# Head norms of a retention branch: the inverse root by ScalarE's root, or by a bit guess and three Newton steps on VectorE

## The chip, the cores and the metric

The kernel runs on one NeuronCore of a Trainium2 chip. The engines named here are TensorE (PE in the profile; its weight loads are PEld), VectorE (DVE), ScalarE (ACT), GpSimd (POOL) and the DMA queues that SyncE issues (SP, SPq). Each engine takes its instructions in the order in which they were written into its queue. The metric is the time of one execution in device microseconds.

## The reference, cut to what matters

One decoder layer is computed for a prompt of 1024 tokens and for 8 samples of 4 tokens. Its input projection feeds two branches: sparse attention (8 heads, the 256 best keys by an indexer), and retention (8 heads). The change lies in the norm of the retention heads. Each head's 64 outputs of a token are brought to mean 0 and variance 1, and then gated:

```python
def _head_norm(o):
    mu = jnp.mean(o, axis=-1, keepdims=True)
    var = jnp.mean(jnp.square(o - mu), axis=-1, keepdims=True)
    return (o - mu) * lax.rsqrt(var + EPS)

    ob, sp = _retention(qb, kb, vb, ...)           # chunks of 128 tokens, state carried on
    yb = jax.nn.silu(gb) * _head_norm(ob)
    y = jnp.einsum('btd,...', concat(ya, yb), w_out)
```

Everything is in float32.

## The kernel before, in words

The kernel is written as tiles and instructions for named engines. A planner turns the program text into one queue for each engine: it plays the program through on a model of the chip (`schedule_with_timeline_sim=True`, line 2002), and whenever an engine is free there, it takes the ready instruction that comes first in the program text, or one that was marked as urgent. So the order in a queue depends on the modelled times of everything ahead of it.

Stages, in order of time: norms of the inputs, the projections for the indexer and attention, the index scores and the search for the thresholds; then the retention stage with the sample branch's key selection; then attention; then the output projection and the gate.

In the retention stage the heads are worked in four pairs (`for hp in range(4)`, line 1566). For each pair:

- `pqk`: eight blocks of 128 tokens are projected to q and k (`mm_a`, lines 287 to 289, 24 matmuls a block), turned by the rotary angle on VectorE (`rope`, lines 1116 to 1118) and finished on GpSimd (1120, 1121).
- `pvg`: the same eight blocks are projected to v and the gate. `take_vg` (1129, 1131) scales v and computes the gate's SiLU on ScalarE.
- The retention itself, block by block (`chunk_mm` and lines 1605 to 1618): q and k are transposed, copied (`qkT`, line 1142), multiplied, masked on VectorE (`sm`, 1148), joined with the carried state (`sbd`, 1610), and the block's 128 outputs for two heads are copied by ScalarE into `acc` (line 1618). A block holds one of three PSUM banks until that copy is done. The state makes the blocks a chain.
- The samples' block (`ret_sample`) fills `acc[:, 8]`.
- The norm. For pairs 0 to 2 `norm_gate` is called twice: for the eight prompt blocks (16 head columns, `nh` = 16, tiles of 128x16) and for the samples (`nh` = 2, tiles of 32x2). VectorE takes mean and variance (1157, 1158), adds epsilon (`gv`, 1163), ScalarE takes the root (1166), VectorE the reciprocal (1167) and one Newton step (1171 to 1181), and the bias (1179 or 1182). Then ScalarE scales three columns in four in place (1186), VectorE the fourth (1188), GpSimd multiplies by the gate (1191), and SP stores `acc` to DRAM (`yb_d`, 1192). There is one `acc`, so the next pair's first copy (1618) waits until both stores have read it.
- For pair 3 nothing is normed there: `acc` and the gates are stored as they are, `last_factors` (lines 1198 to 1214) computes mean and inverse root of its 18 columns, and `last_norm` applies them during attention.

While this runs, VectorE also does the sample branch's selection (`sample_select`, lines 1288 to 1418: scans, compares and prefix sums over 128x2048, and the slot lists at 1380 to 1394), one step of it after each block.

ScalarE's functions come in table sets. A load of a set (ACT_TABLE_LOAD in the profile) stands ahead of the instruction whose function isn't in the set at hand; its line is that instruction's. SiLU and the root are in different sets.

Of the kernel before, what the change touches and what calls it, by code (L numbers as in the profile page):

```python
# [14 lines left out]
I32 = mybir.dt.int32  # L15
U16 = mybir.dt.uint16
AF = mybir.ActivationFunctionType
ALU = mybir.AluOpType
# [113 lines left out]
def tile_step(ctx: ExitStack, tc: tile.TileContext, I, O):  # L132
    nc = tc.nc
# [376 lines left out]
    with pool("ix", side="right") as ix:  # L510
# [131 lines left out]
        for i in range(4):  # L642
            nc.vector.tensor_scalar(place[:, i * 256:i * 256 + 256], C("slots"), i * 256.0, -1.0e-36,
                                    op0=ALU.add, op1=ALU.mult)
# [489 lines left out]
    def chunk_mm(qk, vv, tb, rows, mask_ap, hp):  # L1134
# [13 lines left out]
            nc.vector.tensor_tensor(sm[:rows, j, :rows], sc, mask_ap, op=ALU.mult)  # L1148
        return r, qkT, sm

    def norm_gate(acc, sgs, ntb, rows, tb0, hp):

        nh = ntb * 2
        mv = rt.tile([128, 16, 2], F32, tag="mv", bufs=2, name="bmv")
        for i in range(nh):
            st = rt.tile([128, 6], F32, tag="st", bufs=4, name="bst")
            nc.vector.bn_stats(st[:rows, :], acc[:rows, i // 2, (i % 2) * 64:(i % 2) * 64 + 64])
            nc.vector.bn_aggr(mv[:rows, i, :], st[:rows, :])
        v = rt.tile([128, 16], F32, tag="gv", bufs=1, name="gv")
        y = rt.tile([128, 16], F32, tag="gy", bufs=1, name="gy")  # L1160
        z = rt.tile([128, 16], F32, tag="gz", bufs=1, name="gz")
        v_, y_, z_ = v[:rows, :nh], y[:rows, :nh], z[:rows, :nh]
        nc.vector.tensor_tensor(v_.rearrange("p (t h) -> p t h", h=2),
                                mv[:rows, :nh, 1].rearrange("p (t h) -> p t h", h=2),
                                epsn[:rows, tb0:tb0 + ntb, 2 * hp:2 * hp + 2], op=ALU.add)
        nc.scalar.activation(y_, v_, AF.Sqrt)
        nc.vector.reciprocal(y_, y_)
        one = [slice(i, i + 1) for i in range(nh)]
        if nh == 2:
            for i in one:  # L1170
                nc.vector.tensor_scalar(z_[:, i], y_[:, i], y_[:, i], v_[:, i], op0=ALU.mult, op1=ALU.mult)
        else:
            nc.vector.tensor_tensor(z_, y_, y_, op=ALU.mult)
            nc.vector.tensor_tensor(z_, z_, v_, op=ALU.mult)
        nc.vector.tensor_scalar(z_, z_, -0.5, 1.5, op0=ALU.mult, op1=ALU.add)
        if nh == 2:
            for n, i in enumerate(one):
                nc.vector.tensor_scalar(y_[:, i], y_[:, i], z_[:, i], None, op0=ALU.mult)
                nc.vector.tensor_scalar(z_[:, i], mv[:rows, n, 0:1], y_[:, i], -1.0, op0=ALU.mult, op1=ALU.mult)
        else:  # L1180
            nc.vector.tensor_tensor(y_, y_, z_, op=ALU.mult)
            nc.vector.scalar_tensor_tensor(z_, mv[:rows, :nh, 0], -1.0, y_, op0=ALU.mult, op1=ALU.mult)
        for i in range(nh):
            a = acc[:rows, i // 2, (i % 2) * 64:(i % 2) * 64 + 64]
            if i % 4 < 3:
                nc.scalar.activation(a, a, AF.Identity, bias=z_[:, i:i + 1], scale=y_[:, i:i + 1])
            else:
                nc.vector.tensor_scalar(a, a, mv[:rows, i, 0:1], y_[:, i:i + 1],
                                        op0=ALU.subtract, op1=ALU.mult)
        for t in range(ntb):  # L1190
            nc.gpsimd.tensor_tensor(acc[:rows, t, :], acc[:rows, t, :], sgs[t][:rows], op=ALU.mult)
        nc.sync.dma_start(yb_d[:rows, tb0:tb0 + ntb, hp, :], acc[:rows, :ntb, :])

    wif = wi.rearrange("p t h -> p (t h)")
    lmv, lrs = wif[:, :36].rearrange("p (i c) -> p i c", c=2), wif[:, 36:54]
    nc.gpsimd.memset(lmv[:, 16:, :], 1.0)

    def last_factors(acc):

        for i in range(18):  # L1200
            n = 128 if i < 16 else NS
            st = rt.tile([128, 6], F32, tag="st", bufs=4, name="bst")
            nc.vector.bn_stats(st[:n, :], acc[:n, i // 2, (i % 2) * 64:(i % 2) * 64 + 64])
            nc.vector.bn_aggr(lmv[:n, i, :], st[:n, :])
        v = rt.tile([128, 18], F32, tag="gv", bufs=1, name="gv")
        z = rt.tile([128, 18], F32, tag="gz", bufs=1, name="gz")
        nc.vector.tensor_tensor(v.rearrange("p (t h) -> p t h", h=2),
                                lmv[:, :, 1].rearrange("p (t h) -> p t h", h=2), epsn[:, :, 6:8], op=ALU.add)
        nc.scalar.activation(lrs, v, AF.Sqrt)
        nc.vector.reciprocal(lrs, lrs)  # L1210
        nc.vector.tensor_tensor(z, lrs, lrs, op=ALU.mult)
        nc.vector.tensor_tensor(z, z, v, op=ALU.mult)
        nc.vector.tensor_scalar(z, z, -0.5, 1.5, op0=ALU.mult, op1=ALU.add)
        nc.vector.tensor_tensor(lrs, lrs, z, op=ALU.mult)

    smask = C("smask", 32)
    bmask = C("bmask")
# [348 lines left out]
    for hp in range(4):  # L1566
# [67 lines left out]
        if hp < 3:  # L1634
            norm_gate(acc, sgs, 8, 128, 0, hp)
            norm_gate(acc[:, 8:9, :], [sgS], 1, NS, 8, hp)
        else:
            nc.sync.dma_start(yr_d[:NS, 8, 1], sgS[:NS])
            nc.sync.dma_start(yr_d[:NS, 8, 0], acc[:NS, 8])
            last_factors(acc)  # L1640
# [75 lines left out]
    for qb in range(8):  # L1716
# [6 lines left out]
        n = (qb + 1) * 128  # L1723
# [4 lines left out]
        for kv in range(2):  # L1728
# [5 lines left out]
            for i4 in range(4):  # L1734
# [4 lines left out]
                least, i = 3.0e38, 0  # L1739
                for c in range(0, n, 512):  # L1740
# [5 lines left out]
                    for x0, x1, add in ((c, cut, mask[:, OFF.get(qb, 0) + c:OFF.get(qb, 0) + cut]),  # L1746
                                        (cut, c + wc, near[:, h - 4 * kv, cut - n + 256:c + wc - n + 256])):
                        if x1 > x0:
                            latest[0] = nc.vector.tensor_tensor_reduce(  # L1749
                                L[:, x0:x1], s[:, x0 - c:x1 - c], add, 1.0, least,  # L1750
                                op0=ALU.add, op1=ALU.min, accum_out=mn[:, i:i + 1]).ins
                            least, i = mn[:, i:i + 1], i + 1
# [186 lines left out]
    for cb in range(4):  # L1939
        cur, curu = wg, wu  # L1940
        cs = slice(cb * 256, (cb + 1) * 256)
        for tb in (8, *range(8)):
            rows = 128 if tb < 8 else NS
# [62 lines left out]
```

## Time and profile before

| | us |
|---|---|
| median of three runs (lowest, highest) | 1011.24 (1006.64, 1012.78) |
| the profiled execution's own time | 1009.07 |
| its span, first to last instruction | 1007.0 |
| PE busy, DVE busy | 945.4, 664.2 |
| ACT busy, POOL busy | 453.5, 338.8 |
| mean granted TensorE clock | 0.969 |

The retention stage lies between about 300 and 605 us of the span, and the norms of its four pairs at about 384, 454, 531 and 602 us. In lines of the profile, `gy<-gv` means that the tile `gy` is written from `gv`; a bracket at the end of a row tells how long the engine was idle before it and what ended that.

### The profile page before, as it was taken

To read this page: it belongs to the slowest core of one execution; us is meant where nothing else is said; L and a number is where in the kernel's file an instruction comes from. 1 tells how busy PE (TensorE), PEld (TensorE's weight loads), DVE (VectorE), ACT (ScalarE), POOL (GpSimd) and SP (SyncE) were. 2 spreads that over 40 slices of the span, in tenths; PEclk is the share of its full clock that TensorE was granted. 3 is DMA by queue.
4 is the path that set the end of the run, shared out by engine and by line. 5 is a ranking of instruction groups with operands and counts; after the bars stand their busy time and mean duration, and the time that the engine had idled before them with its cause. 6 is when DMAs were issued, how large, how long until landed. Compare 5 with 4: busy or idle time off the path is not lost.

```text
span 1007.0 us, 18956 instructions
## 1 busy us (share of the span) xinstructions
PE 945.4 (94%) x6983; PEld 798.3 (79%) x6983; DVE 664.2 (66%) x1936; ACT 453.5 (45%) x1005; POOL 338.8 (34%) x444
## 2 busy tenths in 40 slices
PE   4999995989999999998899988999999999999998
PEld 3989993557678988988898866566567999999998
DVE  6747667879946669889679558777754323953332
ACT  5645555345324877224422537465554434432210
POOL 4205215112406326247325226454323322233300
PEclk8999998899999999999899968999999999999999
DMA  8323234567534112032013554533221312422211
GB/s 277 100 73 102 100 111 119 188 206 255 182 104 102 41 43 69 20 91 67 24 43 102 135 162 138 163 105 97 63 79 55 112 53 84 143 86 90 86 39 37
DMA packets 102127, 104.36 MB, mean 104 GB/s; under 512 B 22002, under 2 KB 92210, under 8 KB 99602
## 3 DMA queue, kind: packets, MB, share of 16 engines
q1 hardware_dynamic: 96274, 76.93, 25.8%
q0 software_dynamic: 5760, 26.22, 8.4%
q8 instruction: 55, 0.90, 0.4%
q14 instruction: 38, 0.31, 0.1%
HBM read 80.36 MB, written 22.76 MB: 102 GB/s over the span
## 4 chain that ended last, share of the span: by engine, by line
PE 63%; DVE 14%; DMA 9%; issue 8%; POOL 3%; ACT 2%; SPq 1%; DVEq 0%; POOLq 0%; ACTq 0%
PE pb L277 5%; PE pb L278 4%; PE pb L279 4%; PE ob L1772 3%; PE ptp L1764 3%; PE pg L287 3%; PE pg L289 3%; PE pg L288 3%; PE po L287 3%; PE po L288 3%; PE po L289 3%; PE pox L877 2%; DMA kx<-in_cache_kidx,kidx 2%; PE pvg L287 2%; PE pvg L288 2%
## 5 line engine op out<-in xcount | busy, mean ns | idle before, releaser
L1277 POOL DMA_INDIRECT kvs<-in_cache_kv,idx x64 | 64.2, 1004 | 59.0 <-ACT pT L1769 32.0
L287 PE MATMUL pvg<-whi_vgb,xh 128*128 128x256 f32 x256 | 77.0, 301 | 2.5 <-DVE rp L1118 2.5
L288 PE MATMUL pvg<-wlo_vgb,xh 128*128 128x256 f32 x256 | 75.8, 296 | 0.8 <-POOL wlo_vgb L197 0.8
L287 PE MATMUL pqk<-whi_qkb,xh 128*128 128x256 f32 x256 | 73.8, 288 | 1.5 <-DVE rp L1118 1.2
L289 PE MATMUL pvg<-whi_vgb,xl 128*128 128x256 f32 x256 | 74.6, 292 | 0.0
L287 PE MATMUL po<-whi_o,yTh 128*128 128x256 f32 x256 | 73.3, 286 | 0.4 <-DVE yaT L1783 0.4
L288 PE MATMUL pqk<-wlo_qkb,xh 128*128 128x256 f32 x256 | 73.3, 287 | 0.0
L289 PE MATMUL pqk<-whi_qkb,xl 128*128 128x256 f32 x256 | 73.1, 285 | 0.0
L288 PE MATMUL po<-wlo_o,yTh 128*128 128x256 f32 x256 | 72.9, 285 | 0.0
L287 PE MATMUL pg<-whi_g,yTh 128*128 128x256 f32 x256 | 72.7, 284 | 0.0
L289 PE MATMUL po<-whi_o,yTl 128*128 128x256 f32 x256 | 72.6, 284 | 0.0
L289 PE MATMUL pg<-whi_g,yTl 128*128 128x256 f32 x256 | 72.3, 282 | 0.0
L288 PE MATMUL pg<-wlo_g,yTh 128*128 128x256 f32 x256 | 72.2, 282 | 0.0
L197 POOL TENSOR_TENSOR wlo_g<-wraw_g,whi_g 128x256 fp32r<-128x256 f32 x32 | 27.1, 881 | 88.0 <-ACT whi_g L196 87.9
L1961 DVE TENSOR_TENSOR sgm<-pu,sgm 128x256 f32<-128x256 f32 x32 | 13.6, 424 | 64.5 <-PE pu L289 61.2
L1753 ACT ACTIVATE L<-L,mn 128x128 f32<-128x128 f32 (+7 forms) x64 | 49.6, 777 | 14.5 <-DVE mn L1749 14.1
L543 DVE SCALAR_TENSOR_TENSOR score<-r,wi,score 128x384 f32<-128x384 f32 (+5 forms) x42 | 42.6, 1015 | 20.2 <-ACT r L542 18.2
L287 PEld LDWEIGHTS pvg<-whi_vgb,xh 128*128 128x128 f32 x256 | 50.0, 195 | 4.6 <-issue 2.1
L288 PEld LDWEIGHTS pvg<-wlo_vgb,xh 128*128 128x128 f32 x256 | 50.0, 195 | 1.3 <-POOL wlo_vgb L197 1.0
L287 PEld LDWEIGHTS pqk<-whi_qkb,xh 128*128 128x128 f32 x256 | 48.3, 188 | 3.1 <-issue 2.4
L287 PEld LDWEIGHTS po<-whi_o,yTh 128*128 128x128 f32 x256 | 49.0, 191 | 2.2 <-issue 1.6
L289 PEld LDWEIGHTS pvg<-whi_vgb,xl 128*128 128x128 f32 x256 | 50.1, 196 | 0.3
(559 smaller groups left out, 3115.9 us busy)
## 6 DMA issues: line engine op xcount, KB each, us to landing
wraw_qkb<-in_w_in SPq DMA_DIRECT2D x16, 256.0 KB
wraw_vgb<-in_w_in SPq DMA_DIRECT2D x16, 256.0 KB
wraw_o<-in_w_out SPq DMA_DIRECT2D x8, 512.0 KB
qas<-qas_d SPq DMA_DIRECT2D x8, 512.0 KB
xr<-in_x_prompt SPq DMA_DIRECT2D x8, 512.0 KB
wraw_g<-in_w_ple_gate SPq DMA_DIRECT2D x8, 512.0 KB
out_y_prompt<-sgm SPq DMA_DIRECT2D x32, 128.0 KB
qas_d<-qst SPq DMA_DIRECT2D x8, 384.0 KB
```

The source lines that it names most:

```text
L197: nc.gpsimd.tensor_tensor(lo[:, k, :n], raw, hi[:, k, :n].bitcast(F32), op=ALU.subtract)
L277: nc.tensor.matmul(pt[:m, :n], wh, xh[:, k, ts], start=(k == 0), stop=False)
L278: nc.tensor.matmul(pt[:m, :n], wh, xl[:, k, ts], start=False, stop=False)
L279: nc.tensor.matmul(pt[:m, :n], wl, xh[:, k, ts], start=False, stop=(k == KC - 1))
L287: nc.tensor.matmul(pt[:, :n], ah, hi[:, k, :n], start=(k == 0), stop=False)
L288: nc.tensor.matmul(pt[:, :n], ah, lo[:, k, :n], start=False, stop=False)
L289: nc.tensor.matmul(pt[:, :n], al, hi[:, k, :n], start=False, stop=(k == kc - 1))
L543: nc.vector.scalar_tensor_tensor(sc, r[:, :n], wi[:, qb, h:h + 1], sc if h else place[:, :n], op0=ALU.mult, op1=ALU.add)
L1277: return nc.gpsimd.indirect_dma_start(out=dst, out_offset=None, in_=kvflat, in_offset=bass.IndirectOffsetOnAxis(ap=idx, axis=0))
L1753: behind[0] = nc.scalar.activation(L[:, :n], L[:, :n], AF.Exp, bias=least, scale=-1.0, accum_out=sm[:, i4:i4 + 1])
L1764: nc.tensor.transpose(tp[:, i4 * 128:i4 * 128 + 128], P[i4][:, kb * 128:kb * 128 + 128], ident)
L1772: nc.tensor.matmul(ob[64 * o:64 * o + 64, :256], vtok[:, kb, kv * 64:kv * 64 + 64], pT[:, o * 256:o * 256 + 256], start=(kb == 0), stop=(k ...
```

## The change

A helper `inverse_root(y, z, v)` is added. It takes v's bits as an integer, shifts them right by one, and subtracts that from a constant, which read as a float is a first guess of 1/sqrt(v); three Newton steps follow, of three instructions each. All eleven are on VectorE. `norm_gate` calls it for both shapes in place of ScalarE's root, the reciprocal and the one Newton step, and both shapes now have one instruction for the bias. `last_factors` calls it in the same way. The other norms of the kernel (`rstd_of`, line 253) keep ScalarE's root.

```diff
+    def inverse_root(y, z, v):
+        V = nc.vector
+        V.tensor_scalar(y.bitcast(I32), v.bitcast(I32), 1, None, op0=ALU.logical_shift_right)
+        V.tensor_scalar(y.bitcast(I32), y.bitcast(I32), -1.0, float(0x5F3759DF), op0=ALU.mult, op1=ALU.add)
+        for _ in range(3):
+            V.scalar_tensor_tensor(z, y, -0.5, y, op0=ALU.mult, op1=ALU.mult)
+            V.tensor_tensor(z, z, v, op=ALU.mult)
+            V.scalar_tensor_tensor(y, z, 1.5, y, op0=ALU.add, op1=ALU.mult)
 
     def norm_gate(acc, sgs, ntb, rows, tb0, hp):
...
-        nc.scalar.activation(y_, v_, AF.Sqrt)
-        nc.vector.reciprocal(y_, y_)
-        one = [slice(i, i + 1) for i in range(nh)]
-        if nh == 2:
-            for i in one:
-                nc.vector.tensor_scalar(z_[:, i], y_[:, i], y_[:, i], v_[:, i], op0=ALU.mult, op1=ALU.mult)
-        else:
-            nc.vector.tensor_tensor(z_, y_, y_, op=ALU.mult)
-            nc.vector.tensor_tensor(z_, z_, v_, op=ALU.mult)
-        nc.vector.tensor_scalar(z_, z_, -0.5, 1.5, op0=ALU.mult, op1=ALU.add)
-        if nh == 2:
-            for n, i in enumerate(one):
-                nc.vector.tensor_scalar(y_[:, i], y_[:, i], z_[:, i], None, op0=ALU.mult)
-                nc.vector.tensor_scalar(z_[:, i], mv[:rows, n, 0:1], y_[:, i], -1.0, op0=ALU.mult, op1=ALU.mult)
-        else:
-            nc.vector.tensor_tensor(y_, y_, z_, op=ALU.mult)
-            nc.vector.scalar_tensor_tensor(z_, mv[:rows, :nh, 0], -1.0, y_, op0=ALU.mult, op1=ALU.mult)
+        inverse_root(y_, z_, v_)
+        nc.vector.scalar_tensor_tensor(z_, mv[:rows, :nh, 0], -1.0, y_, op0=ALU.mult, op1=ALU.mult)
...
     def last_factors(acc):
...
-        nc.scalar.activation(lrs, v, AF.Sqrt)
-        nc.vector.reciprocal(lrs, lrs)
-        nc.vector.tensor_tensor(z, lrs, lrs, op=ALU.mult)
-        nc.vector.tensor_tensor(z, z, v, op=ALU.mult)
-        nc.vector.tensor_scalar(z, z, -0.5, 1.5, op0=ALU.mult, op1=ALU.add)
-        nc.vector.tensor_tensor(lrs, lrs, z, op=ALU.mult)
+        inverse_root(lrs, z, v)
```

## The prediction, made before the changed kernel was run

> **What bounds the kernel now.** I read the page first, then the stage of the norms by windows, then who waits there, then single rows. From the page:
>
> ```profile
> span 1007.0 us, 18956 instructions
> PE 63%; DVE 14%; DMA 9%; issue 8%; POOL 3%; ACT 2%; SPq 1%; DVEq 0%; POOLq 0%; ACTq 0%
> ```
>
> The second row is the chain of work that ended last. TensorE carries most of it, VectorE 14%, ScalarE 2%: all of ScalarE's part is about 20 us of 1007, whatever is taken off it. Next, the windows around the four norms (length, then busy time of PE, PEld, DVE, ACT and POOL, the granted clock, DMA):
>
> ```profile
> 377.00:417.00 40.00, 38.37 (x324) 34.96 (x323) 38.07 (x120) 24.38 (x62) 20.89 (x34) 1.00 0.22 55
> 460.00:510.00 50.00, 43.67 (x338) 39.37 (x336) 36.31 (x95) 21.98 (x59) 23.07 (x28) 0.93 0.21 50
> 510.00:565.00 55.00, 51.56 (x451) 46.58 (x450) 51.21 (x205) 20.80 (x54) 26.66 (x43) 0.97 0.43 114
> 565.00:605.00 40.00, 36.02 (x239) 31.63 (x238) 19.68 (x90) 14.27 (x43) 5.51 (x8) 0.76 0.40 114
> ```
>
> Around pair 0 (377 to 417) VectorE is busy 38.07 of 40 us, around pair 2 (510 to 565) 51.21 of 55. ScalarE is busy 24.38 and 20.80. The change moves work from the engine that has room to the one that has little. In the last window the clock is down to 0.76. The chain in order of time says the same of pair 1, and the waits (330 to 605 us; total, times, longest) say what TensorE misses:
>
> ```profile
> 470.73 2.53 DVE cx L1338
> 473.26 0.29 DVE gz L1182
> 473.55 2.78 DVE acc L1188 x4
> ...
> PE second L1147 <- DVE sm L1148: 3.2, 2, 2.3
> PE ret L1147 <- ACT qkT L1142: 1.4, 2, 1.3
> ```
>
> The norm's own bias (`gz`) and scaling (`acc`) stand in the chain of pair 1, among the selection's scans. TensorE waits for VectorE's masks for 3.2 us, and for the copies that ScalarE makes between its loads 1.4 us.
>
> **What comes off ScalarE.** Groups by line (count | busy us, mean ns | idle before):
>
> ```profile
> L1166 ACT ACT_TABLE_LOAD x5 | 6.4, 1283 | 0.1
> L1131 ACT ACT_TABLE_LOAD x5 | 6.4, 1283 | 0.1
> L1209 ACT ACT_TABLE_LOAD x1 | 1.3, 1283 | 0.0
> L1166 ACT ACTIVATE gy<-gv 128x16 f32<-128x16 f32 (+1 forms) x6 | 1.3, 209 | 5.3 <-DVE gv L1163 5.2
> L1209 ACT ACTIVATE wi<-gv 128x18 f32<-128x18 f32 x1 | 0.2, 218 | 0.5 <-DVE gv L1207 0.5
> ```
>
> With no root between the SiLUs the set stays, so 11 loads go, 11 x 1.283 = 14.1 us, and the roots, 1.3 and 0.2: 15.6 us off ScalarE. Whether that shortens anything is read around the loads:
>
> ```profile
> 557.71 0.28 ACT L1131 ACTIVATE sg<-pvg 128x128 f32<-128x128 f32 x1
> 558.00 1.28 ACT L1166 ACT_TABLE_LOAD   x1
> 559.29 0.20 ACT L1166 ACTIVATE gy<-gv 32x2 f32<-32x2 f32 x1
> ...
> 562.59 0.44 ACT L1186 ACTIVATE acc<-acc,gz,gy 32x64 f32<-32x64 f32 x1 [0.61 <-DVE gz L1179]
> ...
> 565.93 0.27 ACT L1618 COPY acc<-ret 128x128 f32<-128x128 f32 x1 [0.74 <-DMA yb_d<-acc]
> ```
>
> A load starts 0.01 us behind the instruction before it and the next one starts 0.01 us behind the load. So a switch costs its 1.28 us here. [...]
>
> The gain at the end of the stage I bound from both sides. Above: the 1.4 us that TensorE waits for ScalarE, and VectorE's wait for the root in this group:
>
> ```profile
> L1167 DVE RECIPROCAL gy<-gy 32x2 f32<-32x2 f32 x3 | 0.4, 148 | 0.4 <-ACT gy L1166 0.4
> ```
>
> That is 1.8 us. Below: nothing, since the work that hides the loads is TensorE's and VectorE's own queue, full in the windows above. I take 1.0, nearer to the upper end because both waits are real. What covers the rest is VectorE; where it thins out (after 565) the loads are already past.
>
> **What comes onto VectorE.** By the diff a prompt call goes from 6 instructions behind `gv` to 12, a samples call from 8 to 12, `last_factors` from 5 to 11: 3 x 6 + 3 x 4 + 6 = 36 more. Their price depends on what stands between them:
>
> ```profile
> 548.65 0.15 DVE L1393 SCALAR_TENSOR_TENSOR row<-row,lo__4954 128x6 f32<-128x6 f32 x1
> 548.73 0.15 DVE L1181 TENSOR_TENSOR gy<-gy,gz 128x16 f32<-128x16 f32 x1
> 548.81 0.41 DVE L1116 TENSOR_TENSOR rp<-pqk,cst 128x256 f32<-128x256 f32 x1
> ...
> 602.10 0.18 DVE L1207 TENSOR_TENSOR gv<-wi,cst 128x18 f32<-128x18 f32 x1
> 602.57 0.27 DVE L1210 RECIPROCAL wi<-wi 128x18 f32<-128x18 f32 x1 [0.28 <-ACT wi L1209]
> ...
> 603.29 0.18 DVE L1213 TENSOR_SCALAR gz<-gz 128x18 f32<-128x18 f32 x1
> 603.50 0.18 DVE L1214 TENSOR_TENSOR wi<-wi,gz 128x18 f32<-128x18 f32 x1
> 603.82 0.29 DVE L1749 CUSTOM_DVE_ANT_0 L<-sa,near 128x128 f32<-128x128 f32 x1
> ```
>
> Among independent work one starts 0.08 us after the other; back to back in one chain, 0.21 us. I take the middle, 0.14. The integer shift and subtraction are not in these rows; I price them as the small float ones. [...]
>
> Pairs 1 and 2 add 20 instructions on an engine that is in the chain there: 20 x 0.14 = 2.8 us (1.6 to 4.2). Pair 0 adds 10 where TensorE and VectorE are both nearly full; I count half, 0.7 us (0 to 2.1).
>
> `last_factors` has a place of its own. Attention's first reduction (603.82, line 1749) is queued behind it on VectorE, and TensorE waits for that:
>
> ```profile
> 604.17 0.47 PE L1743 MATMUL sa<-kahi,qas 128*128 128x128 f32 x1 [2.55 <-DVE mn L1749]
> ```
>
> Now the chain runs from 602.10 to 603.68, with 0.28 us waiting for the root. After, `gv` and eleven dependent ones at 0.21 end at 602.10 + 11 x 0.21 + 0.18 = 604.59: 0.9 us later, all of it on the path (0.6 if they follow at 0.18).
>
> Sum against the profiled execution, 1009.07 us: + 2.8 + 0.7 + 0.9 - 1.0 = + 3.4, which is 1012.5. The least favourable and most favourable ends give + 7.3 and + 0.4: 1016.4 and 1009.5. The three runs' median, 1011.24, lies 2.17 above that execution, so the median may come out up to 1014.7; I forecast 1013.
>
> **The rivals.** Two start from the same place: how early pair 2 lets go of `acc`. The instructions of the norm are far apart on VectorE:
>
> ```profile
> 456.95 0.23 DVE L1167 RECIPROCAL gy<-gy 128x16 f32<-128x16 f32 x1
> ...
> 473.18 0.36 DVE L1182 SCALAR_TENSOR_TENSOR gz<-bmv,gy 128x16 f32<-128x16 f32 x1
> ...
> 535.56 0.16 DVE L1163 TENSOR_TENSOR gv<-bmv,cst 128x16 f32<-128x16 f32 x1
> 538.78 0.23 DVE L1167 RECIPROCAL gy<-gy 128x16 f32<-128x16 f32 x1
> ...
> 550.07 0.44 DVE L1182 SCALAR_TENSOR_TENSOR gz<-bmv,gy 128x16 f32<-128x16 f32 x1
> ```
>
> Five steps take 16.2 us in pair 1 (3.2 each) and 11.3 in pair 2 (2.26 each), because other work is queued between them. And this is what an `acc` that comes late runs into:
>
> ```profile
> 581.55 0.27 PE L1137 MATMUL ret<-cst,qk 128*128 128x128 f32 x1
> ...
> 600.08 0.48 PE L1743 MATMUL sa<-kahi,qas 128*128 128x128 f32 x1
> ...
> 585.00:605.00 20.00, 17.28 (x84) 13.68 (x83) 11.37 (x58) 5.76 (x15) 3.43 (x6) 0.52 0.60 172
> ```
>
> When the last projection is done (581.55), pair 3 still has four blocks and the samples to go, and attention begins at 600.08: 18.5 us for five, 3.7 us each, most of it at a clock of 0.52.
>
> Slower: twelve steps at 2.26 us from 535.56 end at 562.7 instead of 550.07, 12.6 us later. If the pace held, `acc` would come free near 578.5 instead of 565.93, and three more blocks, held in their three banks, would fall behind the last projection: 3 x 3.7 = 11.1 us, with the sum's 3.4 about 1024. It decides from the point where the first copy comes later than the fourth block needs its bank. For it speaks the spacing. Against it: VectorE thins out after 565 (19.68 of 40), and there steps follow at 0.21, so the last ones would catch up.
>
> Faster: today the samples' root waits behind ScalarE's queue until 559.29 and its scaling ends at 563.0, and only then can `acc` be stored and freed at 565.93. On VectorE the samples' chain no longer queues there. If `acc` came free 8 us earlier, two more blocks would run among the projections, 2 x 3.7 = 7.4 us, and the low clock might be half as long: 17.28 us of work at 0.52 would take 9.0 at full clock, half of the 8.3 saved is 4. That gives about 998. Against it: VectorE's order must give way to the samples' chain, and it is the full engine. [...]
>
> No effect: loads and added instructions both lie in gaps, 1008 to 1010. And the planner may put other work between the added instructions than it does now, so that a stall moves from one block to the next, either way; that is in the widths, not a case of its own. That the change would not do what it says (a root left in the stage) the diff excludes: the only roots left are `rstd_of`'s, in the norms before and after this stage.
>
> **How the numbers follow.** The forecast's case, VectorE's price, has 0.42, its own range 1009 to 1017. No effect 0.18. Slower (near 1024) 0.24, faster (near 998) 0.16. The range, 1000 to 1026, reaches into both rivals and leaves out the faster half of the one and the slow end of the other. One per cent, 10 us, is about what a measurement can tell here (the three runs span 6 us). Within it lie the first two cases, 0.60; faster 0.16; slower 0.24.
>
> **What would show it.** Right: no ACT_TABLE_LOAD at lines of the norm or of the SiLU in the pairs; ScalarE 15 us less busy, VectorE about 5 us more; TensorE's wait ahead of attention's second group of scores about 3.5 us instead of 2.55. The slower case would show as more than four blocks of pair 3 behind its last projection and a later first copy into `acc`; the faster as fewer, and less of the clock at a half. I am wrong in kind if the stage from 377 to 605 changes by over 8 us without the number of blocks in that tail changing.

## The result, and the profile after

| | before | after |
|---|---|---|
| median (lowest, highest), us | 1008.94 (1006.28, 1012.78) | 1021.01 (1018.63, 1026.48) |
| profiled execution's own time, us | 1009.07 | 1022.14 |
| its span, us | 1007.0 | 1020.4 |
| DVE busy, ACT busy, us | 664.2, 453.5 | 667.9, 435.3 |

There are four runs on each side. The ratio is 1.0133, with a 95% interval from 1.009 to 1.0176: the change costs some 12 us. ScalarE is 18.2 us less busy, VectorE 3.7 us more. Behind the helper the lines of the changed kernel are 10 lower than before (the copy into `acc` is now line 1608). From its page, the span and the chain of work that ended last:

```profile
span 1020.4 us, 18991 instructions
PE 65%; DVE 14%; DMA 9%; issue 7%; ACT 2%; POOL 2%; SPq 1%; DVEq 0%; ACTq 0%; POOLq 0%
```

Each share is within two points of that of before. Of the groups by line on ScalarE, these are all the table loads that are left:

```profile
L582 ACT ACT_TABLE_LOAD x1 | 1.3, 1283 | 0.7 <-PEq L1984 0.7
L480 ACT ACT_TABLE_LOAD x1 | 1.3, 1283 | 0.0
L1743 ACT ACT_TABLE_LOAD x1 | 1.3, 1283 | 0.0
L259 ACT ACT_TABLE_LOAD x1 | 1.3, 1283 | 0.0
L1944 ACT ACT_TABLE_LOAD x1 | 1.3, 1283 | 0.0
```

None stands at a SiLU (1131) or in the norm: the eleven loads are gone. The windows of the stage after the change, in the columns explained before (start and end, length, busy time and instructions of PE, PEld, DVE, ACT, POOL, granted clock, DMA share, GB/s):

```profile
377.00:417.00 40.00, 36.87 (x311) 33.44 (x311) 37.94 (x126) 19.63 (x52) 22.78 (x35) 1.00 0.22 55
510.00:565.00 55.00, 54.22 (x490) 48.23 (x489) 46.40 (x187) 10.11 (x35) 21.67 (x34) 1.00 0.21 56
565.00:605.00 40.00, 35.21 (x258) 30.98 (x258) 21.98 (x94) 17.51 (x60) 10.66 (x18) 0.96 0.66 183
585.00:605.00 20.00, 16.76 (x113) 13.99 (x112) 11.88 (x45) 7.43 (x23) 5.69 (x8) 0.92 0.60 176
```

The stretch between pair 1's and pair 2's norms, once in the kernel before and once after:

```profile
417.00:510.00 93.00, 85.71 (x690) 77.26 (x688) 72.45 (x207) 32.58 (x90) 38.72 (x47) 0.96 0.22 52
```

```profile
417.00:510.00 93.00, 81.76 (x611) 72.49 (x611) 72.76 (x217) 25.27 (x82) 36.38 (x48) 0.94 0.21 50
```

Here the time goes. Between 417 and 510 us TensorE issues 611 matmuls instead of 690, and between 377 and 417 it issues 311 instead of 324 (some of these because the retention's first copy came 1.3 us later, at 341.3 instead of 340.0, ahead of every norm). Afterwards it catches up a little: 490 instead of 451 up to 565. The clock, which was 0.52 from 585 to 605, is now 0.92 there, but that is no gain: the slow stretch has moved, and from 605 to 640 the clock is now 0.75, where it was 0.93.

Why TensorE is late is to be read from the first copy of each pair into `acc`. Before and after:

```profile
413.44 0.27 ACT L1618 COPY acc<-ret 128x128 f32<-128x128 f32 x1 [2.30 <-DMA yb_d<-acc]
496.31 0.64 ACT L1618 COPY acc<-ret 128x128 f32<-128x128 f32 x3
```

```profile
423.46 0.60 ACT L1608 COPY acc<-ret 128x128 f32<-128x128 f32 x3 [2.08 <-DMA yb_d<-acc]
507.82 0.60 ACT L1608 COPY acc<-ret 128x128 f32<-128x128 f32 x3 [2.06 <-DMA yb_d<-acc]
579.79 0.27 ACT L1608 COPY acc<-ret 128x128 f32<-128x128 f32 x1 [4.54 <-DMA yb_d<-acc]
```

They come 10.0, 11.5 and 13.9 us later than before (565.93 in pair 3, shown in the prediction). Each waits for the store of the pair before it (`yb_d<-acc`), and in pairs 1 and 2 three copies follow at once (x3): all three banks were full and waited (in pair 2 it was so before, too). Why the store is late stands in VectorE's queue. Pair 0's norm before the change, the prompt's variance and bias and the samples' bias:

```profile
385.80 0.15 DVE L1163 TENSOR_TENSOR gv<-bmv,cst 128x16 f32<-128x16 f32 x1
...
391.95 0.16 DVE L1182 SCALAR_TENSOR_TENSOR gz<-bmv,gy 128x16 f32<-128x16 f32 x1
...
409.79 0.31 DVE L1179 TENSOR_SCALAR gz<-bmv,gy 32x1 f32<-32x1 f32 x2
```

After the change, from the variance (line 1173) to the two biases (1177), with some of what is queued between:

```profile
387.16 0.15 DVE L1173 TENSOR_TENSOR gv<-bmv,cst 128x16 f32<-128x16 f32 x1
...
391.63 0.70 DVE L1157 SCALAR_TENSOR_TENSOR gz<-gy 128x16 f32<-128x16 f32 x1
392.25 1.35 DVE L1004 TENSOR_SCALAR sjk<-Xt,ssm 128x2080 uint16<-128x2080 uint16 x1
393.52 0.16 DVE L1158 TENSOR_TENSOR gz<-gz,gv 128x16 f32<-128x16 f32 x1
...
394.34 2.37 DVE L1005 SCALAR_TENSOR_TENSOR su<-su,ssm,sjk 128x2080 uint16<-128x2080 uint16 x1
396.63 0.47 DVE L1159 SCALAR_TENSOR_TENSOR gy<-gz,gy 128x16 f32<-128x16 f32 x1
...
405.73 1.59 DVE L1016 COPY apart<-stop 32x8 f32<-32x8 f32 x4
407.35 0.17 DVE L1158 TENSOR_TENSOR gz<-gz,gv 128x16 f32<-128x16 f32 x1
...
407.72 0.14 DVE L1173 TENSOR_TENSOR gv<-bmv,cst 32x2 f32<-32x2 f32 x1
...
408.32 0.15 DVE L1177 SCALAR_TENSOR_TENSOR gz<-bmv,gy 128x16 f32<-128x16 f32 x1
...
420.43 0.15 DVE L1177 SCALAR_TENSOR_TENSOR gz<-bmv,gy 32x2 f32<-32x2 f32 x1
```

Variance and twelve steps, of 0.15 to 0.8 us each, take 21.2 us, where the kernel before took 6.2. The prompt's bias comes 16.4 us later than before, and the samples', behind which the second store stands, 10.6. In pairs 1 and 2 it is 26.0 and 18.8 us from variance to bias, after 17.2 and 14.5. So the delay begins at pair 0's norm: 10.0 of the 13.9 us are there at pair 1's first copy. The planner has put other work between pair 0's steps, and from the second Newton step on that is long: the sample branch's threshold search over 128x2080 (lines 1004 to 1016), the rotary products, the samples' new state. The row at 407.72 shows a second thing. `gv`, `gy` and `gz` have one buffer each, which the prompt's and the samples' call share. The samples' `gv` can be written only when the prompt's last product with `v` has been read, and their `gy` only when ScalarE has done the prompt's scaling. The samples' first and last step in pairs 1 and 2:

```profile
502.53 0.19 DVE L1154 TENSOR_SCALAR gy<-gv 32x2 int32<-32x2 int32 x1 [2.37 <-ACT acc L1181]
504.81 0.15 DVE L1177 SCALAR_TENSOR_TENSOR gz<-bmv,gy 32x2 f32<-32x2 f32 x1
...
570.13 0.19 DVE L1154 TENSOR_SCALAR gy<-gv 32x2 int32<-32x2 int32 x1 [0.61 <-ACT acc L1181]
572.79 0.15 DVE L1177 SCALAR_TENSOR_TENSOR gz<-bmv,gy 32x2 f32<-32x2 f32 x1
```

There VectorE waits for ScalarE, and then the twelve steps follow one another in 2.3 and 2.7 us. Last, the wait at attention's second group of scores:

```profile
614.23 0.48 PE L1733 MATMUL sa<-kahi,qas 128*128 128x128 f32 x1 [3.46 <-DVE mn L1739]
```

### The profile page after: what moved, and what is told of

The parts are those of the page before. It is cut to its first block, busy times and chain, and to the rows that moved or that the text cites. A ratio compares the mean times of both kernels' runs of the same rounds, so it can differ in the third digit from the quotient of the medians.

```text
span 1020.4 us, 18991 instructions
## 1 busy us (share of the span) xinstructions
PE 948.6 (93%) x6983; PEld 797.3 (78%) x6983; DVE 667.9 (65%) x1972; ACT 435.3 (43%) x987; POOL 337.0 (33%) x444
## 4 chain that ended last, share of the span: by engine, by line
PE 65%; DVE 14%; DMA 9%; issue 7%; ACT 2%; POOL 2%; SPq 1%; DVEq 0%; ACTq 0%; POOLq 0%
PE pb L277 4%; PE pb L278 4%; PE pb L279 4%; PE ob L1762 4%; PE ptp L1754 4%; PE pg L287 3%; PE pg L289 3%; PE pg L288 3%; PE pvg L287 3%; PE pox L877 2%; PE pvg L288 2%; PE pvg L289 2%; PE po L287 2%; PE po L288 2%; PE po L289 2%
## 5 line engine op out<-in xcount | busy, mean ns | idle before, releaser
L543 DVE SCALAR_TENSOR_TENSOR score<-r,wi,score 128x384 f32<-128x384 f32 (+5 forms) x42 | 42.6, 1015 | 18.7 <-ACT r L542 16.6
```

The costliest lines, as they stand in the source:

```text
L543: nc.vector.scalar_tensor_tensor(sc, r[:, :n], wi[:, qb, h:h + 1], sc if h else place[:, :n], op0=ALU.mult, op1=ALU.add)
```

## The experiments

**Theory A**: the longer chain ends later, so both stores come later, `acc` is free later, and the next pair's retention, and with it TensorE, starts later. **Rival B**: 36 more instructions on VectorE, whatever they belong to. **Rival C**: the planner's other order. **Rival D**: `last_factors`, which is on the path. In the table, "copy" is the start of a pair's first copy into `acc`, "attention" that of its first matmul, and ratios are to the kernel before on the same chip, each with its 95% interval. All times but the ratios are from the profiled execution.

| kernel | ratio | copy, pair 1 | pair 2 | pair 3 | attention | span |
|---|---|---|---|---|---|---|
| before | 1 | 413.4 | 496.3 | 565.9 | 600.1 | 1007.0 |
| the change | 1.0133 (1.009 to 1.0176) | 423.5 | 507.8 | 579.8 | 609.2 | 1020.4 |
| pairs_only | 1.0095 (1.0064 to 1.0125) | 424.2 | 509.3 | 581.4 | 612.0 | 1019.2 |
| one_step | 0.9962 (0.9941 to 0.9984) | 415.1 | 495.6 | 567.6 | 597.3 | 1002.1 |
| two_steps | 1.0107 (1.0067 to 1.0146) | 421.6 | 505.8 | 579.7 | 609.2 | 1024.4 |
| idle_work | 1.0037 (1.0013 to 1.0061) | 417.3 | 507.3 | 576.3 | 605.6 | 1013.4 |
| unbroken | 1.0358 (1.0318 to 1.0398) | 434.0 | 518.9 | 602.8 | 634.8 | 1040.8 |
| samples_only | 1.0024 (1.0001 to 1.0046) | 417.9 | 498.5 | 570.4 | 600.5 | 1011.6 |
| prompt_only | 1.0108 (1.0074 to 1.0141) | 424.9 | 511.0 | 582.8 | 612.1 | 1022.0 |
| two_buffers | 1.0115 (1.0077 to 1.0153) | 420.2 | 507.6 | 579.8 | 608.5 | 1022.2 |
| own_tile | 1.0047 (1.0017 to 1.0078) | 418.0 | 504.3 | 576.8 | 605.2 | 1013.4 |
| before_own_tile | 0.9982 (0.9959 to 1.0005) | 410.0 | 492.6 | 568.8 | 597.6 | 1007.0 |
| on_gpsimd | 1.0119 (1.007 to 1.0169) | 422.8 | 510.6 | 584.3 | 613.0 | 1019.3 |
| short_own_tile | 1.0046 (1.0015 to 1.0076) | 421.8 | 502.6 | 575.9 | 606.7 | 1018.9 |

Three columns belong together. In every kernel but the one before, attention starts 28.4 to 32.0 us after pair 3's first copy (34.2 in the kernel before, whose clock was 0.52 from 585 to 605). So the start of pair 3's blocks carries the delay on to attention. In eleven of the fourteen rows the profile names the store of `acc` as what that copy waited for last; in `unbroken`, `on_gpsimd` and `short_own_tile` it names something else or shows no wait. The columns are not exact to a few us: pair 0's first copy, ahead of every norm, comes between 338.8 and 342.2 in these executions, and a profiled execution lies up to 4.1 us off its kernel's median. The rest of the span, from attention on, differs by up to 10.4 us (404.8 in `one_step` to 415.2 in `two_steps`), and not in the order of the release. Nearly all of that lies in attention itself, 144.0 to 154.5 us from the first to the last group of scores, into which more or less of the slow stretch falls; that much of the spans is not explained by the release.

### The last pair's factors alone undone

```diff
     def last_factors(acc):
-        inverse_root(lrs, z, v)
+        nc.scalar.activation(lrs, v, AF.Sqrt)
+        nc.vector.reciprocal(lrs, lrs)
...
```

> The changed kernel, but with the last pair's factors (`last_factors`) worked out as before, by ScalarE's root. Theory A (the twelve-step chain in the first three pairs' norms delays the release of `acc`): the loss stays, 1019 to 1022, only the under 1 us of TensorE's longer wait ahead of attention's second group of scores comes back. Rival D (the last pair's factors are what costs, since they stand on the path): the time is back at 1009 to 1011.

1.0095, with an interval that overlaps the change's. The pairs' norms bring most of the loss, and rival D, as the whole cause, falls. TensorE's longer wait in attention, 3.46 instead of 2.55 us, is the 0.9 us that was expected, and it is gone in this kernel (2.53); the ratios are too wide to show it.

### One Newton step, and two

```diff
-        for _ in range(3):
+        for _ in range(1):
```

> The changed kernel with one Newton step instead of three (six instructions fewer in each norm's chain and in the last pair's factors; it leaves out two Newton steps, so the roots are only good to some 0.2%). Theory A (length of the chain): with half the steps the chain is no longer than that of the kernel before, first copies into `acc` in pairs 2 and 3 are back near 496 and 566 us, and the time is 1006 to 1011. Theory B (it is VectorE's busy time): 42 instructions fewer are 42 x 0.09 to 0.14 = 4 to 6 us less, 1015 to 1017. Rival C (another order of the planner's, whatever the length): anything from 1009 to 1022, and the first copies' times don't follow the length.

> The changed kernel with two Newton steps instead of three (three instructions fewer in each call; it leaves out the third step). Theory A: between the change and the kernel with one step, first copies of pairs 2 and 3 near 502 and 574 us, 1009 to 1015. Rival B (instructions alone, 0.1 us each): 21 fewer than the change, 1016 to 1019. Rival C (order): not between the two.

With one step the kernel is faster than the kernel before, by 0.4%, and the first copies are back where they were. With two steps it is as slow as with three. So the price isn't proportional to the number of steps: 21 instructions fewer gained nothing measurable, 21 further ones gained 1.4%. Pair 0 shows why. The bias (1177) with one step, and the chain's last product and bias with two:

```profile
390.92 0.33 DVE L1159 SCALAR_TENSOR_TENSOR gy<-gz,gy 128x16 f32<-128x16 f32 x1
...
391.84 0.16 DVE L1177 SCALAR_TENSOR_TENSOR gz<-bmv,gy 128x16 f32<-128x16 f32 x1
391.93 1.51 DVE L1004 TENSOR_SCALAR sjk<-Xt,ssm 128x2080 uint16<-128x2080 uint16 x1
```

```profile
393.34 0.16 DVE L1158 TENSOR_TENSOR gz<-gz,gv 128x16 f32<-128x16 f32 x1
396.44 0.47 DVE L1159 SCALAR_TENSOR_TENSOR gy<-gz,gy 128x16 f32<-128x16 f32 x1
...
401.81 0.16 DVE L1177 SCALAR_TENSOR_TENSOR gz<-bmv,gy 128x16 f32<-128x16 f32 x1
```

With one step the chain is through 0.09 us before the search's long instructions begin (line 1004). A chain of two or three steps is caught by them: 10 us later with two, 16.5 with three. Theory A holds in kind; its number for two steps (1009 to 1015) was wrong, because it took the price per step as even. The length and the planner's order are not told apart here: a short chain is quick because it gets in ahead of the search, and no run has a short chain in a worse place.

### As many instructions, no longer chain

```diff
+        dm = rt.tile([128, 16], F32, tag="dm", bufs=1, name="dm")
+        for _ in range(7 if nh > 2 else 5):
+            nc.vector.tensor_scalar(dm[:rows, :nh], v_, -0.5, 1.5, op0=ALU.mult, op1=ALU.add)
```

> The kernel before, with 36 more small instructions on VectorE at the place of the norms (seven in each prompt call, five in each call of the samples), which read the variances and write a tile that nobody reads. As many instructions as the change adds, but no longer chain. Theory A: 1009 to 1012, the small instructions fill gaps. Theory B (VectorE's time by itself): 1019 to 1022, as the changed kernel. Rival C: anything between.

1.0037, 3.7 us (1.3 to 6.1): some three tenths of the loss. Rival B, as the whole, falls; as a part it stands. It is no purely separate part: the first copy in pair 3 comes 10.4 us later here too, because instructions that nobody reads still stand in the queue ahead of those that the store waits for.

### The chain kept together

```diff
-        inverse_root(y_, z_, v_)
+        with tc.tile_critical():
+            nc.vector.drain()
+            inverse_root(y_, z_, v_, nc.vector.drain)
```

> The changed kernel, with the eleven instructions of a norm's root kept together in VectorE's queue, so that nothing is put between them (a drain of VectorE after each takes the place of the waits among them; `last_factors` as in the change). Theory A: a chain of 11 x 0.25 to 0.4 us = 3 to 4.5 us in place of some 20, the first scales of pairs 1 and 2 at 475 to 485 and 552 to 558 us, and the time back to 1006 to 1013. Theory B: the same work and 12 drains more for each call, 1021 to 1026. Rival C: no particular time.

The miss was the largest of all: 1.0358. The first and last instruction of pair 0's eleven, and the variance that they wait for:

```profile
386.64 0.15 DVE L1178 TENSOR_TENSOR gv<-bmv,cst 128x16 f32<-128x16 f32 x1
...
417.06 0.17 DVE L1154 TENSOR_SCALAR gy<-gv 128x16 int32<-128x16 int32 x1 [2.23 <-PE ret L1602]
...
419.57 0.18 DVE L1163 SCALAR_TENSOR_TENSOR gy<-gz,gy 128x16 f32<-128x16 f32 x1
```

The chain itself took 2.7 us, as expected. But the planner put the block as a whole 30.4 us behind its input, after other work and an idle 2.23 us. So the test wasn't the one that was meant. It still tells something: with as many steps, in an eighth of the time, the kernel is slower still. In pair 1 the first copy waits for a later store, as in the change (434.00). In pairs 2 and 3 it doesn't wait for the store, so there the blocks kept whole and their drains cost in another way, which the rows don't show. At pair 0 it isn't the length of the chain that counts, but when its last instruction comes.

### Samples' calls alone, prompt's calls alone

```diff
+        if nh == 2:
+            inverse_root(y_, z_, v_)
...
+        else:
+            nc.scalar.activation(y_, v_, AF.Sqrt)
...
```

So `samples_only`; `prompt_only` has the condition `nh > 2`. Both leave `last_factors` as before the change.

> The kernel before with the new root in the samples' calls alone (the prompt's calls and the last pair's factors by ScalarE's root). Theory A with the chains in series: ScalarE's root waited 8 us behind other work there, and the new chain of twelve instructions takes 2 to 6 us once the tiles are free, so the samples' scales come no later than before, 1004 to 1010. Rival (the samples' chain is the dear part, as it stands last before `acc` is free): 1015 to 1020.

> The kernel before with the new root in the prompt's calls alone (the samples' calls and the last pair's factors by ScalarE's root). Theory A: the prompt's chain is where VectorE's queue is full, so most of the loss is here, 1014 to 1019 (7 to 10 us of the 12, since the samples' calls alone gave 2). Rival H (the loss needs both chains, one behind the other on the same tiles): 1009 to 1012.

0.24% and 1.08%. The prompt's calls bring most of the loss and need no help from the samples' chain: rival H falls. With both kinds of calls (`pairs_only`) it is 0.95%, so the samples' chain adds nothing that can be measured.

### The single buffers

```diff
-        v = rt.tile([128, 16], F32, tag="gv", bufs=1, name="gv")
+        v = rt.tile([128, 16], F32, tag="gv", bufs=2, name="gv")
...
```

The same for `gy` and `gz`, and in `last_factors`.

> The changed kernel with two buffers instead of one for each of the norm's small tiles (`gv`, `gy`, `gz`), so that the samples' chain needn't wait for the last reads of the prompt's. As much work on VectorE as in the change. Theory A, with the two chains in series as part of its price: the samples' scales come 4 to 6 us earlier (near 500 and 568 us in pairs 1 and 2), `acc` is free that much earlier, 1012 to 1018. Rival B (VectorE's instructions alone, which the kernel with idle work put at some 4 us, and the prompt's long chain): the series of the two costs nothing, 1018 to 1022.

No gain. That the two chains stand one behind the other on the same tiles is real (the bracket of 2.37 us above), but it is not what costs: with two buffers the samples' scales still stand behind the prompt's on ScalarE, and start only 1.3 us earlier in pair 1 (503.7 instead of 505.0) and 1.7 us in pair 2 (571.3 instead of 573.0). In pair 0 they start 3.5 us earlier (417.1 instead of 420.6) and pair 1's first copy comes 3.2 us earlier, but at pair 1's norm nothing of that is left: the prompt's bias comes at 497.82 instead of 497.68. And in pair 3 another wait takes over. The stores' issues and pair 3's first copy in this kernel:

```profile
570.51 4.14 SPq L1187 DMA_DIRECT2D yb_d<-acc  x2
```

```profile
579.80 0.43 ACT L1608 COPY acc<-ret 128x128 f32<-128x128 f32 x2 [4.00 <-DMA yb_d<-acc]
```

And in the change, the queue of DMAs and the window behind it:

```profile
565.78 1.24 SPq L1642 DMA_DIRECT2D kalo<-ka_d  x2
567.12 1.63 SPq L186 DMA_DIRECT2D wraw_o<-in_w_out  x2
570.74 0.37 SPq L1187 DMA_DIRECT2D yb_d<-acc  x1
...
575.53 0.38 SPq L1187 DMA_DIRECT2D yb_d<-acc  x1
```

```profile
570.00:575.00 5.00, 5.00 (x40) 4.54 (x40) 3.20 (x17) 3.56 (x17) 1.16 (x3) 1.00 1.07 243
```

In the change the second store's issue starts at 575.53 and the copy at 579.79. With two buffers that issue starts at 572.59 and ends at 574.65 (570.51 + 4.14), and the copy starts at 579.80. Loads for attention and for the output projection were issued just ahead, and the DMA engines are full (a share of 1.07). What was gained ahead of the store is lost again behind it. The profile doesn't tell which of the two stores landed last: the prompt's was issued at 570.74 in the change and at 570.51 with two buffers, 9.1 and 9.3 us ahead of the copy, and it alone may have held the copy in pair 3.

### The samples' rows in a tile of their own

```diff
-        acc = rt.tile([128, 9, 128], F32, tag="acc", bufs=1, name=f"acc{hp}")
+        acc = rt.tile([128, 8, 128], F32, tag="acc", bufs=1, name=f"acc{hp}")
+        accS = rt.tile([128, 1, 128], F32, tag="accS", bufs=1, name=f"accS{hp}")
```

> The changed kernel with the samples' rows in a tile of their own instead of the ninth block of `acc`, so that the next pair's copies wait for the prompt's store alone, and not for the samples' chain behind it. Theory A (the release of `acc` sets the next pair's start): first copies of pairs 2 and 3 some 5 us earlier than in the change (near 504 and 574 us), 1010 to 1016. Rival B (VectorE's instructions and not the release): 1018 to 1022, although the first copies come earlier.

> The kernel before with the samples' rows in a tile of their own and nothing else. Control for the run of the changed kernel with that tile. Theory A: before the change the samples' store follows the prompt's by 5 to 12 us and its landing releases `acc`, so here too there is something to gain, the first copies of pairs 1 to 3 come some 2 to 8 us earlier and the time is 1000 to 1008. Rival G (the release isn't what TensorE waits for in the kernel before): 1007 to 1011, the same.

With the change's twelve steps left as they are, the first copies come 5.5, 3.5 and 3.0 us earlier, and the ratio is 1.0047. In pair 3 its copy waits for the prompt's store alone, 8.5 us from the issue:

```profile
568.34 0.37 SPq L1187 DMA_DIRECT2D yb_d<-acc  x1
```

```profile
576.84 0.43 ACT L1609 COPY acc<-ret 128x128 f32<-128x128 f32 x2 [4.61 <-DMA yb_d<-acc]
```

Timed beside it on the same chip, the kernels with two steps and with two buffers gave 1.0107 and 1.0115. This is the direct test of the release, and it speaks for theory A, though the gain isn't the release alone: the prompt's biases of pairs 1 and 2 come 3.5 and 3.8 us earlier than in the change (494.14 and 562.03), for which the rows give no cause, and of the 7.0 us between the spans 3.0 lie behind attention's start. The control says where the effect ends: the kernel before gains nothing that can be measured (0.9982, interval to 1.0005), though its copies in pairs 1 and 2 come 3.5 and 3.7 us earlier. It is no clean control, since pair 3's comes 2.9 us later. With `samples_only`, whose copies come 2.2 to 4.5 us later at a ratio of 1.0024, it speaks for some slack in the kernel before, which the change used up. The work of the 36 more instructions is still there, 0.37% as measured above, which is about the size of the 0.47% that are left here.

A second `acc` would take the wait away altogether; no run has one.

### The chain on GpSimd

```diff
-        V.tensor_scalar(y.bitcast(I32), v.bitcast(I32), 1, None, op0=ALU.logical_shift_right)
-        V.tensor_scalar(y.bitcast(I32), y.bitcast(I32), -1.0, float(0x5F3759DF), op0=ALU.mult, op1=ALU.add)
+        V.tensor_scalar(y.bitcast(I32), v.bitcast(I32), -0.5, float(0x5F3759DF), op0=ALU.mult, op1=ALU.add)
...
-        inverse_root(y_, z_, v_)
+        inverse_root(y_, z_, v_, nc.gpsimd)
```

> The changed kernel with the root of the three pairs' norms worked out by GpSimd instead of VectorE: the guess in one instruction (the bits read as a number, times -0.5, plus the constant) and three Newton steps of four instructions, 13 dependent steps where the change has 11; `last_factors` keeps VectorE, with the guess in one instruction. Theory A (a dependent chain between whose steps VectorE's full queue puts other work): GpSimd's queue is thin there, its smallest instructions take 0.21 us, so 13 steps take 3 to 8 us in place of some 20, first scales of pairs 1 and 2 near 476 to 484 and 552 to 558 us, 1003 to 1011. Rival E (the number of dependent steps by itself, on whatever engine): 1018 to 1024. Rival B (VectorE's instructions alone: fewer than before the change by some 6 per prompt call): 1004 to 1008.

The prompt's chain got shorter, though less than expected: the first scales of pairs 0, 1 and 2 start at 397.0, 488.4 and 560.9 instead of 408.5, 497.9 and 566.0. Yet the kernel is as slow as the change. The samples' chain on GpSimd in pair 2, its second instruction, its third and its last:

```profile
572.72 0.24 POOL L1155 TENSOR_TENSOR gz<-gy 32x2 f32<-32x2 f32 x1
573.11 0.96 POOL L1266 DMA_INDIRECT kvs<-in_cache_kv,idx  x1 [0.15 <-DVE rp L1118]
...
574.92 0.19 POOL L1156 TENSOR_TENSOR gz<-gz,gv 32x2 f32<-32x2 f32 x1
577.68 0.96 POOL L1266 DMA_INDIRECT kvs<-in_cache_kv,idx  x1 [2.57 <-DVE idx L1383]
...
581.12 0.18 POOL L1158 TENSOR_TENSOR gy<-gy,gz 32x2 f32<-32x2 f32 x1
```

It stands behind the rotary work and the gathers for attention, and one of these waits 2.57 us for VectorE's indices; the chain's fourth instruction, whose input was done at 575.11, comes only behind it, at 578.66. The samples are stored at 582.85, and pair 3's first copy comes at 584.30, later than in the change. Theory A in the form "VectorE's queue, and nothing else, makes the chain slow" falls; that the last of the two stores sets the time holds once more.

### A short chain with a tile of its own

```diff
-        for _ in range(3):
+        for _ in range(2):
```

With it the guess in one instruction, as on GpSimd, and `accS` as above.

> The changed kernel with the guess in one instruction and two Newton steps (seven dependent instructions for eleven; it leaves out the third Newton step), in all five kinds of calls, and the samples' rows in a tile of their own. Theory A: the chain is between those of the kernels with one and with two steps, and the release of `acc` doesn't wait for the samples, 1003 to 1010. Rival F (what made the kernel with one step quick was the planner's order, not the length; the kernel with two steps was no quicker than the change): 1014 to 1020.

1.0046, no better than `own_tile` with its eleven steps; the expected time was missed, and rival F, the planner's order, isn't excluded. Pair 0's first scale is at 401.7: the chain is still caught by the search's instructions. No kernel with two or more Newton steps beats the kernel before. Only `one_step` does, by 0.4%, and it leaves out the accuracy.

## Why the prediction was right or wrong

Forecast 1013, range 1000 to 1026; measured 1021.0. The range held it, but the sum did not: it had + 3.4 us, and some 12 came. The range reached so far only because the slower rival, with 0.24, was let into it; that was not the forecast's mechanism. (The sum's least favourable end is + 7.2 and not + 7.3: 4.2 + 2.1 + 0.9.)

- **ScalarE's relief.** Eleven loads and the roots, 15.6 us, were to go; 18.2 went. Its gain on the path, taken at 1.0 us, isn't seen alone. `one_step`, with no loads and 6 instructions fewer than before on VectorE, gains 3.6 us on medians of 1003.9 and 1007.5, and the fewer instructions are in that too, so the loads' own part is likely smaller. One of the eleven loads, at line 1209, did not lie ahead of 565, as the prediction has it, but at 600.49.
- **The price of the instructions.** 2.8 + 0.7 = 3.5 us for the pairs. `idle_work`, with 36 independent ones, measured 3.7 us (1.3 to 6.1). The size was right. The integer shift and the subtraction, priced as small float ones, take 0.15 to 0.17 us in five of their twelve rows of the pairs' norms, 0.19 to 0.71 in the others, and 0.17 each where the chain was kept together (`unbroken`, pair 0). Steps that follow one another lie 0.18 us apart at 32x2 (pair 2, five steps from 572.06 to 572.79). What the chain cost, 21.2 us in pair 0, had little to do with these durations.
- **`last_factors`.** + 0.9 us, from 2.55 to about 3.5 us ahead of the second group of scores: 3.46. Size and mechanism were right.
- **The step that failed** is "Pairs 1 and 2 add 20 instructions ...: 20 x 0.14 = 2.8 us", and with it pair 0's 0.7 us. It prices the engine's time for the added steps and leaves out that the last of them ends later, by whatever is queued between. That term, the later release of `acc`, was put into the slower rival alone. It is most of the loss, and by the first copies most of it begins at pair 0: its prompt's bias came 16.4 us later, and pair 1's first copy 10.0 (1.3 of these were there ahead of the norm).
- **The slower rival** had the mechanism and its size: the norm's steps at the pace of the queue, and the first copy of pair 3 near 578.5; it came at 579.79. It was wrong in place. It expected three more blocks behind pair 3's last projection. After the change there are four, as before (copies at 597.98, 599.40, 606.25 and 607.96), because the projections had become late as well (the last one from 581.43 to 591.49): most of the loss had happened in pair 1, where three full banks waited for the copy that pair 0's norm held up. Its counter-argument, that the last steps would catch up where VectorE thins out, was right for the samples' steps (0.18 us apart), and no help for the prompt's, which come earlier.
- **The faster rival** saw the samples' root freed from ScalarE's queue. `samples_only` shows what that is worth: nothing, 1.0024.
- **"Wrong in kind"** if the stage changed by over 8 us without the number of blocks in that tail changing: attention's first matmul moved from 600.08 to 609.22, 9.1 us, and there are still four. Of the 9.1 us, 1.3 were there ahead of 377, which leaves 7.8, so the test as it was put falls just short. Wrong in kind the case was all the same, by the step above.
- **The planner's order**, counted as a width and not as a case: `unbroken` has the change's arithmetic, and its placement, with the drains, added some 23 us (1.0358 against 1.0133). As a mere width it was too small.

What stays open: how the loss divides between the chain's end and the added instructions, since the latter also delay the former; how far a chain's length and the planner's order can be told apart; and why attention itself takes over 10 us longer in one execution than in another.

## What to carry to other kernels

Price an added step in a dependent chain by when the chain's last instruction comes, and not by the instruction's own time. In the full queue here, the spacing of the steps in the trace before, times their number, put pair 2's bias at 562.7, and it came at 565.82; and pair 0's jumped by 10.0 us from one Newton step to two, where the chain ran into a stretch of long instructions. Then ask what waits for that last instruction, and how much slack it has; here a single buffer waited, through a store. Work taken off an engine that is 45% busy and has 2% of the chain that ended last (ScalarE) brought next to nothing here, though it was 18 us.

## What was not expected of the hardware

A switch of function tables that costs 1.28 us of ScalarE eleven times could go without a gain that a ratio shows as its own. A chain whose eleven instructions take 2.7 us when nothing stands between (`unbroken`, pair 0) took 21.2 us from variance to bias in the queue, and an engine with room (GpSimd, 33% busy) made the prompt's chain shorter (`on_gpsimd`: first scales 5.1 to 11.5 us earlier) and the samples' longer (in pair 2, 8.4 us from its second instruction to its last, where the change's twelve steps take 2.7). And a store of 512 KB, issued behind other loads, took 8.5 us from its issue to the copy that waited for it alone (`own_tile`, pair 3).
